# Token sums of a Strassen-like product: x1 and x2 in PSUM, issued in four parts behind the products of the chunk in front; modulation steps there left out or thinned

## The chip, the cores and the metric

The kernel runs on one core of a Trainium2 chip. The metric is the device time of one execution in microseconds (us). The engines are named as the profile names them: PE (TensorE, matmul; PEld its weight loads), DVE (VectorE), ACT (ScalarE), POOL (GpSimd) and SP (SyncE, which issues DMAs). Each engine runs its own instructions in a fixed order.

## The reference

Two layers of a generator over 512 latent tokens and 256 context tokens, model width 1024, all in float32. Each layer is a half SwiGLU feed-forward, a token mixer (neighbourhood attention in layer 0, windowed attention in layer 1), and a second half SwiGLU. Every sub-layer is modulated by shift, scale and gate that come from a conditioning vector, and ends in a layer norm.

```python
def modulate(h, shift, scale):
    return h * (1.0 + scale) + shift

def swiglu(u, w_in, w_out):
    a, v = jnp.split(u @ w_in, 2, axis=-1)
    return (jax.nn.silu(a) * v) @ w_out

def ffn_sublayer(h, shift, scale, gate, w_in, w_out, g, b):
    y = swiglu(modulate(h, shift, scale), w_in, w_out)
    return layer_norm(ALPHA * h + FFN_RES * gate * y, g, b)

for i in range(DEPTH):                       # DEPTH = 2
    m_lat = split(silu(c) @ w_mod[i] + b_mod[i], 9)      # and m_ctx from c_ctx
    h = ffn_sublayer(h, m[0], m[1], m[2], ffn_w_in[i, 0], ffn_w_out[i, 0], ...)
    ...                                      # mixer i, layer norm
    h = ffn_sublayer(h, m[6], m[7], m[8], ffn_w_in[i, 1], ffn_w_out[i, 1], ...)
```

The hidden width of a feed-forward is 2816.

## The kernel before, in words

Tokens lie along the free axis, features along the 128 partitions. A float32 value goes to PE as two parts, high and low (`uh`, `ul` for the activations, `wh`, `wl` for the weights, `gh`, `gl` for the gated product), and each product is three matmuls (`mm3`, L146 to L148).

There are four feed-forwards, `0a`, `0b`, `1a` and `1b`. The first three take 768 tokens in two groups, 512 and 256 wide; `1b` takes the 512 latent tokens in two groups of 256. A feed-forward is a loop over `NCH` = 11 chunks of 256 hidden columns. A chunk first computes `a` and `v` for its two column halves and its groups (function `av`: tiles `pa`, `pv`; SiLU on ACT; the product with `v` on DVE, L456; the split into `gh` and `gl`, L457 and L458), and then multiplies by `w_out` (function `down`: 16 tiles `pd`; each is added to the stream `z` by `accumulate`, L432 on DVE). Inside `1b` one of the eight stream tiles is called `zspare`.

Chunks 0 up to `s0` - 1 run in this plain way; `s0` is 3 in `0a` and 2 in the others. Chunks `s0` to 8 run as `seven`: a Strassen-like form with seven products (`p0` to `p6`) in place of eight. It needs sums of quarters of the weights (`quarters`, tiles `S`, POOL, L541, split by ACT L102 and POOL or DVE L104) and sums of quarters of the activations. The latter are made once for each feed-forward:

- `sums()`, at the top of chunk `s0` - 1. For each of four rows `j` it stores the odd half of `uh` and `ul` in DRAM (two DMAs on SP), then makes x1 (three DVE instructions, L490), x3 (three POOL instructions, L490) and x2 from x1 (two DVE instructions, L490). Each of the three is split by a copy on ACT (L511) and a subtraction on DVE (L512) into tiles `T`. x1, x2 and x3 lie in the scratch tiles `t2` in SBUF, of which there are six.
- `fourth()`, at the end of chunk `s0` - 1: two subtractions on POOL (L523), an addition on DVE (L524), a copy on ACT (L525) and a subtraction on DVE (L526) for each row, in place over the odd half of `uh` and `ul`.

Product `p2` needs x2, `p3` x1, `p5` x3, `p6` what `fourth()` leaves. A set of these sums is 32 DVE, 12 POOL and 12 ACT instructions in `sums()` and 8 of each in `fourth()`, of 384 columns each, in `1b` of 256.

PSUM has eight banks, two of them tagged `mm`, two `s`, two `c`, one `t`, one `o`. `av` uses `mm` and `c`. Downs of chunks 1 to 8 and the seven products take `mm`, `s` and `c` in turn (`next_bank`).

Beside the feed-forwards `0a`, `0b` and `1a` the modulation vectors of what follows are computed on DVE (`gemv_dve`, L198: one multiply-and-sum of 128x512 for each step, with its accumulator read). The steps wait in a list `bg`; `tick()` takes from it as many as `pace` says, four times in a plain chunk and 14 times in a `seven` chunk. `weight` says how much of the work a chunk gets:

```python
weight = [0] + [1.6] * (s0 - 1) + [1.0] * (NCH - 2 - s0)
each = sum(n + 1 for n, _ in bg) / (sum(weight) - 0.1)
pace[0] = each * weight[ci] / (4 if ci < s0 else 14)
```

`0a` has 193 such entries, `0b` 97, `1a` 130 and `1b` none. `each` is thus 21.2, 11.4 and 15.3 before.

The order of the instructions on each engine is not written out by hand. A planner takes them by program order, when their inputs and a free buffer are there by its own model of times, so that an instruction may be put ahead of an earlier one. `behind(x, y)` forbids this for two instructions of the same engine: `x` then stands after `y`. It does nothing where the engines differ. `last[0]` is the last accumulate, gated product or combining step on DVE that the program has issued so far; the modulation steps stand behind it.

Of the kernel before, what the change touches and what calls it, by code (L numbers as in the profile page):

```python
# [8 lines left out]
F32 = mybir.dt.float32  # L9
F32R = mybir.dt.float32r  # L10
# [3 lines left out]
ALU = mybir.AluOpType  # L14
# [4 lines left out]
P = 128  # L19
# [7 lines left out]
NCH = NF // 2  # L27
# [11 lines left out]
def hybrid_kernel(ctx: ExitStack, tc: tile.TileContext, h0, cc, crow, wmod, wmodt, bmod, lnp, wst,  # L39
                  rpbp, nmask, sinks, ropec, rmat, ident, wmask, out):  # L40
    nc = tc.nc
# [5 lines left out]
    dp = ctx.enter_context(tc.tile_pool(name="dp", bufs=1, space=DRAM))  # L47
    banks = {"mm": 2, "s": 2, "c": 2, "t": 1, "o": 1}

    def bank(tag, nm):  # L50
        return pp.tile([P, 512], F32, tag=tag, name=nm, bufs=banks[tag])

    def t2(nm, tag="t2"):
        return tp.tile([P, 512], F32, tag=tag, name=nm, bufs={"t2": 6, "ln": 2, "sl": 2}[tag])
# [25 lines left out]
    uh = [rp.tile([P, NT], F32R, name=f"uh{d}") for d in range(DT)]  # L80
    ul = [rp.tile([P, NT], F32R, name=f"ul{d}") for d in range(DT)]
# [27 lines left out]
    ph, phase_of = {}, [None, ExitStack()]  # L109
# [76 lines left out]
    bg, last, last_exp, wtq = [], [None], [None], [0]  # L186
# [36 lines left out]
    def tick():  # L223

        pace[1] += pace[0]
        while bg and pace[1] >= 1:
            pace[1] -= 1
            if next(bg[0][1], "end") == "end":
                bg.pop(0)
# [78 lines left out]
    def behind(x, y):  # L308

        if y is not None and x.ins.engine == y.ins.engine:  # L310
            tc.add_manual_dep(x.ins, y.ins.name, mybir.DependencyInfo(
                mybir.DependencyClass.NoSync, mybir.DependencyReason.DATA), reason="order")
# [123 lines left out]
    def ffn(nm, groups, gt, mid, post, units=(), opened={}, head=None, apart=None):  # L436
# [4 lines left out]
        def unit(slabs=False):  # L441
            return units.pop(0) if units else wunit(slabs)
# [34 lines left out]
        n2 = nb * P  # L477

        def half(t, h):

            return t[:, 0:nb * 256].rearrange("p (a s b) -> p s a b", s=2, b=P)[:, h]

        def as_half(t):
            return t.rearrange("p (a b) -> p a b", b=P)

        ts = [[[None, None] for _ in range(4)] for _ in range(3)]

        def op(eng, out, a, b, o):
            a, b = [half(y[0], y[1]).bitcast(F32) if isinstance(y, tuple) else as_half(y) for y in (a, b)]
            eng.tensor_tensor(out=as_half(out), in0=a, in1=b, op=o)  # L490

        def sums():


            saved = dp.tile([2, 4, P, n2], F32, name=f"sv{nm}")
            for j in range(4):
                for x, t in enumerate((uh, ul)):
                    nc.sync.dma_start(saved[x, j].rearrange("p (a b) -> p a b", b=P), half(t[j], 1).bitcast(F32))
                x1, x2, x3 = [t2(f"x{nm}_{j}_{i}")[:, 0:n2] for i in range(3)]
                k = j + 4  # L500
                op(nc.vector, x1, (uh[j], 1), (uh[j], 0), ALU.subtract)
                op(nc.vector, x1, x1, (ul[j], 1), ALU.add)
                op(nc.vector, x1, x1, (ul[j], 0), ALU.subtract)
                op(nc.gpsimd, x3, (uh[k], 1), (uh[j], 1), ALU.subtract)
                op(nc.gpsimd, x3, x3, (ul[k], 1), ALU.add)
                op(nc.gpsimd, x3, x3, (ul[j], 1), ALU.subtract)
                op(nc.vector, x2, (uh[k], 1), x1, ALU.subtract)
                op(nc.vector, x2, x2, (ul[k], 1), ALU.add)
                for i, x in enumerate((x1, x2, x3)):
                    hi, lo = [ph["T"].tile([P, 384], F32R, tag=f"T{i}{j}{y}", name=f"T{nm}_{i}_{j}{y}", bufs=1)[:, 0:n2] for y in "hl"]  # L510
                    nc.scalar.copy(hi, x)  # L511
                    nc.vector.tensor_tensor(out=lo, in0=x, in1=hi.bitcast(F32), op=ALU.subtract)  # L512
                    ts[i][j] = [as_half(hi), as_half(lo)]
            return saved

        def fourth():

            for j in range(4):
                x = t2(f"x{nm}_{j}_4")[:, 0:n2]
                k = j + 4  # L520
                for i, (a, b, o) in enumerate(((ts[1][j][0], half(uh[k], 0), ALU.subtract), (ts[1][j][1], half(ul[k], 0), ALU.subtract))):
                    y = x if i == 0 else t2(f"x{nm}_{j}_5")[:, 0:n2]
                    nc.gpsimd.tensor_tensor(out=as_half(y), in0=a.bitcast(F32), in1=b.bitcast(F32), op=o)  # L523
                nc.vector.tensor_tensor(out=x, in0=x, in1=y, op=ALU.add)  # L524
                nc.scalar.copy(half(uh[j], 1), as_half(x))  # L525
                nc.vector.tensor_tensor(out=half(ul[j], 1), in0=as_half(x), in1=half(uh[j], 1).bitcast(F32), op=ALU.subtract)  # L526

# [73 lines left out]
        if mid is not None:  # L601
            mid()
        gts.append(gt())
        late_downs = []
        s0 = 3 if opened else 2
        weight = [0] + [1.6] * (s0 - 1) + [1.0] * (NCH - 2 - s0)
        each = sum(n + 1 for n, _ in bg) / (sum(weight) - 0.1)
        for ci in list(range(NCH)) + [("r", NCH - 2)]:
            r = isinstance(ci, tuple)
            if not r and 0 < ci < NCH - 2:  # L610
                phase("T")
                pace[0] = each * weight[ci] / (4 if ci < s0 else 14)
                if ci == s0 - 1:
                    saved = sums()
            if not r and s0 <= ci < NCH - 2:
                gs = [[gp.tile([P, NT], F32R, tag="gs", name=f"g{x}{nm}_{ci}_{i}", bufs=6) for x in "hl"] for i in range(2)]

                def lagging(ci=ci, gs=gs, u=wpos[0] + 2):
                    w = wunit(again=u, adding=True)
                    if ci == NCH - 3:  # L620
                        restore(saved)
                    for g in ([(0, NL, 0)] if nb == 2 else groups):
                        down(w, f"{ci}", gs, g, True)

                for i in range(2):
                    seven(f"{nm}_{ci}_{i}", wpos[0] + i, *gs[i])
                    while i == 0 and late_downs:
                        late_downs.pop()()
                late_downs.append(lagging)
                wpos[0] += 3  # L630
                if ci == NCH - 3:
                    late_downs.pop()()
                if ci == NCH - 3:
                    pace[0] = 1
                    while bg:
                        tick()
                continue
            if ci == NCH - 2:
                phase("S")
            late = ci == NCH - 2  # L640
            if late:
                again = wpos[0]
            w = [wunit(again=again + i) if r else unit(i == 2 and (ci == NCH - 1 or ci == 0 and apart is not None)) for i in range(3)]
            cn = f"r{ci[1]}" if r else f"{ci}"
            gs = [[gp.tile([P, NT], F32R, tag="gs", name=f"g{x}{nm}_{cn}_{i}", bufs=6) for x in "hl"] for i in range(2)]

            def avs(*todo):
                for g, i in todo:
                    av(w[i], f"{cn}_{i}", g, *gs[i], opened.get((i, g)) if ci == 0 else None, 4 if late else 0)
                    if not r and 0 < ci < s0:  # L650
                        tick()

            def dn(g):
                down(w[2], cn, gs, g, not r and 0 < ci < NCH - 2)

            a, b = groups
            if r:
                avs((b, 0), (b, 1))
                dn(b)
                post(1)  # L660
            elif late:
                avs((a, 0), (a, 1))
                dn(a)
            elif ci == NCH - 1:
                avs((a, 0), (a, 1))
                dn(a)
                avs((b, 0), (b, 1))
                post(0)
                dn(b)
            elif ci == 0 and apart:  # L670
                apart()
                avs((head[0], 0), (head[0], 1))
                dn(head[0])
                avs(*[(g, i) for g in head[1:] for i in range(2)])
                for g in head[1:]:
                    dn(g)
            else:
                avs(*([(g, i) for g in head for i in range(2)] if ci == 0 else [(a, 0), (b, 0), (a, 1), (b, 1)]))
                dn(a)
                dn(b)  # L680
            if ci == s0 - 1:
                fourth()
            if mid is not None and ci == 1:
                bias_tables()
# [424 lines left out]
    with tc.tile_pool(name="pre", bufs=1) as fp:  # L1109
        open_av()  # L1110
        for q in range(4):
            pieces = []
            for i in range(2):
                t = fp.tile([P, 4, 512], F32, tag="wm", name=f"wm0_{q}_{i}", bufs=7)
# [196 lines left out]
```

## Time and profile before

| | |
|---|---|
| runs | 2860.72, 2865.42, 2865.66 us, median 2865.42 |
| profiled execution, its own time | 2863.12 us |
| span of the profiled execution | 2861.0 us |
| mean granted PE clock | 0.977 |
| busy: PE, DVE, POOL, ACT | 2716.4, 1820.9, 1675.4, 1218.0 us |
| HBM traffic | 322.15 MB, mean 113 GB/s |

In rows of instructions a group reads: line, engine, operation, out<-in tiles, shapes, count | busy us, mean ns of one | idle time of the engine before them, and what ended it. In rows of stretches, each engine's busy time in the stretch is followed by the number of its instructions, and the row ends with the granted PE clock, the share of the DMA engines and GB/s; where the row is for one line of the code, only the engines that run this line are named. In rows of waits stands who waited for whom, how many us in total, how often, and the longest. Buffer numbers are left out of tile names, so that the chunks of one feed-forward share a name and are told apart by time.

### The profile page before, as it was taken

To read this page: it belongs to the slowest core of one execution; us is meant where nothing else is said; L and a number is where in the kernel's file an instruction comes from. 1 tells how busy PE (TensorE), PEld (TensorE's weight loads), DVE (VectorE), ACT (ScalarE), POOL (GpSimd) and SP (SyncE) were. 2 spreads that over 40 slices of the span, in tenths; PEclk is the share of its full clock that TensorE was granted. 3 is DMA by queue.
4 is the path that set the end of the run, shared out by engine and by line. 5 is a ranking of instruction groups with operands and counts; after the bars stand their busy time and mean duration, and the time that the engine had idled before them with its cause. 6 is when DMAs were issued, how large, how long until landed. Compare 5 with 4: busy or idle time off the path is not lost. (4 is left out here: it accounts for less than half of the span.)

```text
span 2861.0 us, 48069 instructions
## 1 busy us (share of the span) xinstructions
PE 2716.4 (95%) x17122; PEld 2438.8 (85%) x17122; DVE 1820.9 (64%) x4122; ACT 1218.0 (43%) x2496; POOL 1675.4 (59%) x1488
## 2 busy tenths in 40 slices
PE   8999999999999979999999889999997999899997
PEld 5789999888888868899998779999886777789997
DVE  3597776375555677766553886666457767787744
ACT  4224433266446343333433424433336655444543
POOL 4547674475434445876644667676456545577763
PEclk9999999999999989999999999999999999999998
DMA  8465656232221213445452335656431111135562
GB/s 300 124 192 159 159 144 162 79 99 78 56 56 54 66 49 93 118 126 137 116 140 77 93 107 142 169 169 181 133 97 47 51 38 45 56 88 134 126 174 70
DMA packets 285871, 322.15 MB, mean 113 GB/s; under 512 B 28480, under 2 KB 174016, under 8 KB 284608
## 3 DMA queue, kind: packets, MB, share of 16 engines
q1 hardware_dynamic: 269792, 290.63, 34.5%
q0 software_dynamic: 15552, 28.32, 6.0%
q8 instruction: 135, 2.21, 0.3%
q14 instruction: 104, 0.85, 0.1%
q10 hardware_dynamic: 288, 0.14, 0.0%
HBM read 311.14 MB, written 12.25 MB: 113 GB/s over the span
## 5 line engine op out<-in xcount | busy, mean ns | idle before, releaser
L104 POOL TENSOR_TENSOR wl<-wr,wh 128x512 fp32r<-128x512 f32 x308 | 406.0, 1333 | 307.7 <-ACT wh L102 268.8
L104 POOL TENSOR_TENSOR wl_s<-S,wh_s 128x512 fp32r<-128x512 f32 x202 | 270.4, 1374 | 49.5 <-ACT wh_s L102 44.1
L102 ACT CAST wh<-wr 128x512 fp32r<-128x512 f32 x308 | 187.7, 621 | 228.6 <-DMA wr<-in_wst_dram 59.4
L102 ACT CAST wh_s<-S 128x512 fp32r<-128x512 f32 x216 | 132.1, 622 | 325.2 <-POOL S L541 80.9
L541 POOL TENSOR_TENSOR S<-wr,wr 128x512 f32<-128x512 f32 x108 | 147.5, 1366 | 172.7 <-DMA wr<-in_wst_dram 147.7
L198 DVE CUSTOM_DVE_ANT_0 jk<-wt,cb 128x512 f32<-128x512 f32 x278 | 185.3, 680 | 57.8 <-DMA wt<-in_wmodt_dram 56.2
L104 POOL TENSOR_TENSOR wl_a<-wr,wh_a 128x512 fp32r<-128x512 f32 x120 | 159.2, 1382 | 31.8 <-ACT wh_a L102 22.3
L102 ACT CAST wh_a<-wr 128x512 fp32r<-128x512 f32 x162 | 100.8, 623 | 133.5 <-PE pd1b L147 17.0
L432 DVE SCALAR_TENSOR_TENSOR z<-pd0b,gt,z 128x256 f32<-128x256 f32 (+1 forms) x176 | 102.7, 602 | 63.1 <-PE pd0b L148 62.9
L432 DVE SCALAR_TENSOR_TENSOR z<-pd1a,gt,z 128x512 f32<-128x512 f32 (+1 forms) x168 | 99.0, 620 | 41.1 <-PE pd1a L148 40.8
L432 DVE SCALAR_TENSOR_TENSOR z<-pd0a,gt,z 128x512 f32<-128x512 f32 (+1 forms) x168 | 98.0, 619 | 34.4 <-PE pd0a L148 34.2
L765 POOL TENSOR_SCALAR p<-p,l 128x512 f32<-128x512 f32 x64 | 44.3, 694 | 119.4 <-DVE l L863 111.0
L305 POOL TENSOR_SCALAR z<-z,ag_None,ab_None 128x256 f32<-128x256 f32 (+1 forms) x78 | 68.8, 888 | 67.0 <-DVE uh L291 65.3
L198 DVE CUSTOM_DVE_ANT_0 jk<-zspare,cb 128x512 f32<-128x512 f32 x138 | 92.7, 680 | 13.6 <-DMA zspare<-in_wmodt_dram 13.4
L765 POOL TENSOR_SCALAR pw<-pw,l 128x512 f32<-128x512 f32 (+1 forms) x64 | 40.9, 641 | 66.2 <-DVE l L1052 25.4
L541 POOL TENSOR_TENSOR S<-S,wr 128x512 f32<-128x512 f32 x54 | 77.2, 1430 | 4.2 <-DVE x0b L524 1.7
L541 POOL TENSOR_TENSOR S<-wr,S 128x512 f32<-128x512 f32 x54 | 76.5, 1416 | 4.0 <-DVE ul L526 0.6
L862 ACT ACTIVATE p<-s,m 128x512 f32<-128x512 f32 x64 | 44.1, 690 | 77.7 <-DVE m L860 72.7
L287 ACT ACTIVATE ufl<-z,bi_None,sc_None 128x256 f32<-128x256 f32 (+1 forms) x86 | 54.5, 657 | 34.3 <-DVE z L411 33.9
L432 DVE SCALAR_TENSOR_TENSOR z<-pd1b,gt,z 128x512 f32<-128x512 f32 (+1 forms) x98 | 56.5, 610 | 13.2 <-PE pd1b L148 11.0
L292 DVE TENSOR_TENSOR ul<-ufl,uh 128x256 fp32r<-128x256 f32 (+1 forms) x88 | 60.4, 696 | 0.9 <-ACT ufl L287 0.6
L146 PE MATMUL pd0a<-gh0a,wh 128*128 128x512 f32 (+1 forms) x144 | 50.3, 358 | 8.0 <-DVE z L432 7.8
(1462 smaller groups left out, 10701.1 us busy)
## 6 DMA issues: line engine op xcount, KB each, us to landing
wr<-in_wst_dram SPq DMA_DIRECT2D x524, 256.0 KB
wt<-in_wmodt_dram SPq DMA_DIRECT2D x160, 256.0 KB
zspare<-in_wmodt_dram SPq DMA_DIRECT2D x80, 256.0 KB
wr_0b<-in_wst_dram SPq DMA_DIRECT2D x42, 256.0 KB
wr_1b<-in_wst_dram SPq DMA_DIRECT2D x42, 256.0 KB
wr_2b<-in_wst_dram SPq DMA_DIRECT2D x42, 256.0 KB
wr_3b<-in_wst_dram SPq DMA_DIRECT2D x42, 256.0 KB
wm<-in_wmod_dram SPq DMA_DIRECT2D x8, 1024.0 KB
```

What stands on the lines that cost most here:

```text
L102: nc.scalar.copy(hi[:], src[:])
L104: eng.tensor_tensor(out=lo[:], in0=src[:], in1=hi[:].bitcast(F32), op=ALU.subtract)
L146: nc.tensor.matmul(ps, a[0], b[0], start=first, stop=False)
L198: x = nc.vector.tensor_tensor_reduce(out=junk[:], in0=w[:], in1=cb[st], scale=1.0, scalar=0.0, op0=ALU.mult, op1=ALU.add, accum_out=acc[:, ...
L287: nc.scalar.activation(uf[:, :n], zs, AF.Identity, scale=s1, bias=s2)
L292: return hi, nc.vector.tensor_tensor(out=lo, in0=uv, in1=uo.bitcast(F32), op=ALU.subtract)
L305: nc.gpsimd.tensor_scalar(out=zs, in0=zs, scalar1=prm[2][:, d:d + 1], scalar2=prm[3][:, d:d + 1], op0=ALU.mult, op1=ALU.add)
L432: last[0] = nc.vector.scalar_tensor_tensor(out=zt(d, c0, c1), in0=pd, scalar=gt[:, d, st:st + 1], in1=zt(d, c0, c1), op0=ALU.mult, op1=ALU ...
L541: nc.gpsimd.tensor_tensor(out=t[:], in0=a[:], in1=b[:], op=o)
L765: nc.gpsimd.tensor_scalar(out=p, in0=p, scalar1=r, scalar2=0.0, op0=ALU.mult, op1=ALU.add)
L862: last_exp[0] = nc.scalar.activation(p[:], ps[:], AF.Exp, bias=m[:, 0:1], scale=-1.0, accum_out=l[:, 0:1])
```

## The change

1. x1 and x2 lie in PSUM (banks `s`) and no more in `t2`; x3 stays in `t2`. In `fourth()` the sum lies in a bank `s` and its two inputs in `t2`.
2. `sums()` is called for one row at a time: row 0 at the top of chunk `s0` - 1, rows 1 to 3 after the first three `av` of this chunk. The 16 storing DMAs are issued together before row 0 (`save`).
3. The instructions of the sums on DVE stand behind `last[0]`.
4. Modulation steps: `weight` is 0 for chunk 1 in `0b` and `1a`; in `0a` it is 1.3 for chunk 1 and 0.7 for chunk 2, in place of 1.6 each. `each` becomes 24.4, 14.1 and 18.8 in `0a`, `0b` and `1a`, so that the later chunks take more.

```diff
@@ in ffn
         def op(eng, out, a, b, o):
             a, b = [half(y[0], y[1]).bitcast(F32) if isinstance(y, tuple) else as_half(y) for y in (a, b)]
-            eng.tensor_tensor(out=as_half(out), in0=a, in1=b, op=o)
-
-        def sums():
-            saved = dp.tile([2, 4, P, n2], F32, name=f"sv{nm}")
+            behind(eng.tensor_tensor(out=as_half(out), in0=a, in1=b, op=o), last[0])
+
+        def save(saved):
             for j in range(4):
                 for x, t in enumerate((uh, ul)):
                     nc.sync.dma_start(saved[x, j].rearrange("p (a b) -> p a b", b=P), half(t[j], 1).bitcast(F32))
-                x1, x2, x3 = [t2(f"x{nm}_{j}_{i}")[:, 0:n2] for i in range(3)]
+
+        def sums(j):
+            x1, x2 = [bank("s", f"x{nm}_{j}_{i}")[:, 0:n2] for i in range(2)]
+            x3 = t2(f"x{nm}_{j}_2")[:, 0:n2]
+            k = j + 4
+            op(nc.vector, x1, (uh[j], 1), (uh[j], 0), ALU.subtract)
+            op(nc.vector, x1, x1, (ul[j], 1), ALU.add)
+            op(nc.vector, x1, x1, (ul[j], 0), ALU.subtract)
+            op(nc.gpsimd, x3, (uh[k], 1), (uh[j], 1), ALU.subtract)
+            op(nc.gpsimd, x3, x3, (ul[k], 1), ALU.add)
+            op(nc.gpsimd, x3, x3, (ul[j], 1), ALU.subtract)
+
+            def split(i, x):
+                hi, lo = [ph["T"].tile([P, 384], F32R, tag=f"T{i}{j}{y}", name=f"T{nm}_{i}_{j}{y}", bufs=1)[:, 0:n2] for y in "hl"]
+                nc.scalar.copy(hi, x)
+                behind(nc.vector.tensor_tensor(out=lo, in0=x, in1=hi.bitcast(F32), op=ALU.subtract), last[0])
+                ts[i][j] = [as_half(hi), as_half(lo)]
+
+            op(nc.vector, x2, (uh[k], 1), x1, ALU.subtract)
+            op(nc.vector, x2, x2, (ul[k], 1), ALU.add)
+            split(0, x1)
+            split(1, x2)
+            split(2, x3)
+
+        def fourth():
+            for j in range(4):
+                x = bank("s", f"x{nm}_{j}_3")[:, 0:n2]
                 k = j + 4
...
-                for i, (a, b, o) in enumerate(((ts[1][j][0], half(uh[k], 0), ALU.subtract), (ts[1][j][1], half(ul[k], 0), ALU.subtract))):
-                    y = x if i == 0 else t2(f"x{nm}_{j}_5")[:, 0:n2]
-                    nc.gpsimd.tensor_tensor(out=as_half(y), in0=a.bitcast(F32), in1=b.bitcast(F32), op=o)
-                nc.vector.tensor_tensor(out=x, in0=x, in1=y, op=ALU.add)
+                ys = [t2(f"x{nm}_{j}_{i}")[:, 0:n2] for i in (4, 5)]
+                for i, t in enumerate((uh, ul)):
+                    nc.gpsimd.tensor_tensor(out=as_half(ys[i]), in0=ts[1][j][i].bitcast(F32), in1=half(t[k], 0).bitcast(F32),
+                                            op=ALU.subtract)
+                nc.vector.tensor_tensor(out=x, in0=ys[0], in1=ys[1], op=ALU.add)
                 nc.scalar.copy(half(uh[j], 1), as_half(x))
                 nc.vector.tensor_tensor(out=half(ul[j], 1), in0=as_half(x), in1=half(uh[j], 1).bitcast(F32), op=ALU.subtract)
...
-        late_downs = []
+        late_downs, js = [], [1, 2, 3]
         s0 = 3 if opened else 2
-        weight = [0] + [1.6] * (s0 - 1) + [1.0] * (NCH - 2 - s0)
+        weight = [0] + [1.3] * (s0 - 2) + [0.7 * (s0 - 2)] + [1.0] * (NCH - 2 - s0)
...
                 if ci == s0 - 1:
-                    saved = sums()
+                    saved = dp.tile([2, 4, P, n2], F32, name=f"sv{nm}")
+                    save(saved)
+                    sums(0)
...
                     if not r and 0 < ci < s0:
                         tick()
+                    if not r and ci == s0 - 1 and js:
+                        sums(js.pop(0))
```

More of the change, by code (lines that the diff above doesn't have):

```diff
@@ L498, in sums @@
                     nc.sync.dma_start(saved[x, j].rearrange("p (a b) -> p a b", b=P), half(t[j], 1).bitcast(F32))
-                x1, x2, x3 = [t2(f"x{nm}_{j}_{i}")[:, 0:n2] for i in range(3)]
[L500 to L513, printed above, removed]
@@ L514, in sums @@
-            return saved
+        def sums(j):
[18 more added lines that the diff above has]
+            split(2, x3)
@@ L516, in fourth @@
         def fourth():
             for j in range(4):
-                x = t2(f"x{nm}_{j}_4")[:, 0:n2]
+                x = bank("s", f"x{nm}_{j}_3")[:, 0:n2]
                 k = j + 4
-                for i, (a, b, o) in enumerate(((ts[1][j][0], half(uh[k], 0), ALU.subtract), (ts[1][j][1], half(ul[k], 0), ALU.subtract))):
-                    y = x if i == 0 else t2(f"x{nm}_{j}_5")[:, 0:n2]
-                    nc.gpsimd.tensor_tensor(out=as_half(y), in0=a.bitcast(F32), in1=b.bitcast(F32), op=o)
```

## The prediction

> **What bounds the kernel now.** I read the page first, then the windows of each stage, then what TensorE (PE) waits for, then the timeline of VectorE (DVE) in those places.
>
> ```profile
> PE 2716.4 (95%) x17122; PEld 2438.8 (85%) x17122; DVE 1820.9 (64%) x4122; ACT 1218.0 (43%) x2496; POOL 1675.4 (59%) x1488
> ```
>
> PE is the bound: only 2861.0 - 2716.4 = 145 us of the span have no matmul running. The change can win only where PE stands still or clocks low near the code it touches. The next view gives busy time by stretch: chunks 1 and 2 of `0a`, chunk 1 and then chunk 2 of `0b`, chunk 1 of `1a`, of `1b`; then the down products of one chunk in `0b`, `1a`, `1b` and of a later chunk in `1b`; last the worst stretch of `1a`.
>
> ```profile
> core 0: us, PE busy (x) PEld busy (x) DVE busy (x) ACT busy (x) POOL busy (x), PEclk, DMA share, GB/s
> 105.00:165.00 60.00, 52.45 (x286) 45.33 (x285) 57.28 (x109) 15.22 (x30) 42.95 (x33) 0.94 0.59 170
> 165.00:212.00 47.00, 46.59 (x267) 40.77 (x266) 43.09 (x115) 11.09 (x22) 21.74 (x17) 1.00 0.64 183
> 1120.00:1167.00 47.00, 40.36 (x220) 33.88 (x220) 46.84 (x91) 15.15 (x31) 33.80 (x28) 0.96 0.33 90
> 1167.00:1227.00 60.00, 59.07 (x338) 56.34 (x337) 37.60 (x86) 23.18 (x43) 48.30 (x40) 1.00 0.48 128
> 1680.00:1722.00 42.00, 42.00 (x258) 37.98 (x257) 33.95 (x84) 12.06 (x24) 29.19 (x22) 1.00 0.51 149
> 2506.00:2546.00 40.00, 33.99 (x259) 32.87 (x258) 38.91 (x61) 15.61 (x37) 32.64 (x29) 0.91 0.17 51
> ...
> 1138.60:1165.30 26.70, 20.06 (x98) 15.47 (x97) 26.70 (x53) 7.82 (x16) 20.20 (x16) 0.94 0.27 69
> 1702.20:1719.10 16.90, 16.90 (x98) 14.77 (x98) 16.39 (x32) 3.81 (x8) 14.95 (x12) 1.00 0.42 123
> 2521.90:2542.70 20.80, 14.79 (x98) 13.67 (x97) 19.78 (x33) 7.28 (x16) 16.89 (x15) 0.84 0.13 39
> 2572.80:2584.00 11.20, 11.20 (x51) 9.07 (x50) 7.54 (x13) 3.47 (x8) 9.80 (x8) 1.00 0.60 142
> ...
> 1636.00:1662.00 26.00, 16.47 (x72) 13.23 (x72) 25.94 (x29) 7.20 (x17) 22.64 (x18) 0.74 0.30 87
> ```
>
> See that DVE is full (57.28 of 60, 46.84 of 47, 38.91 of 40, 25.94 of 26) exactly where PE idles, and that the clean stretches have PE at 100% and clock 1.00. The same 16 down tiles of one chunk take 26.70 us in `0b` and 16.90 in `1a`: 9.8 us lost. In `1b` 20.80 against 11.20 (the same 24,576 columns in wider matmuls): 9.6 lost. In `0a` PE idles 60.00 - 52.45 = 7.55, in `1a` 26.00 - 16.47 = 9.53. What PE waits for there, a row each from the waits of 0a, 0b, 1a (two) and 1b:
>
> ```profile
> PE pd0a L146 <- DVE z L432: 7.5, 5, 3.0
> ...
> PE pd0b L146 <- DVE gl0b L458: 3.0, 1, 3.0
> ...
> PE pv1a L146 <- DVE gl1a L458: 6.1, 1, 6.1
> PE pd1a L146 <- DVE z L432: 3.5, 1, 3.5
> ...
> PE pd1b L146 <- DVE zspare L432: 5.0, 1, 5.0
> ```
>
> It waits for accumulates (`z`, L432) and for the split of the gated product (`gl`, L458): short DVE steps queued behind `sums()`. **Removable: 7.55 + 9.8 + 9.53 + 9.6 = 36.5 us.** With the lowered clock of the idle stretches of `0a` and `1a` (52.45 x 0.06 = 3.1 and 16.47 x 0.26 = 4.3) the ceiling is about 44.
>
> **Part 1: x1 and x2 in PSUM.** DVE instructions of these tiles (256 columns where the name ends in `1b`, else 384), by form:
>
> ```profile
> L490 DVE TENSOR_TENSOR x1a<-x1a,ul 128x384 f32<-128x384 f32 x12 | 11.6, 975 | 0.0
> L490 DVE TENSOR_TENSOR x0b<-uh 128x384 f32<-128x384 f32 x4 | 2.2, 548 | 0.0
> L570 DVE TENSOR_TENSOR p51a<-p51a,y1a 128x384 f32<-128x384 f32 x14 | 7.9, 567 | 1.8 <-DVE p51a L570 0.5
> L570 DVE TENSOR_TENSOR y1a<-p11a,y01a 128x384 f32<-128x384 f32 x14 | 7.8, 556 | 21.5 <-PE p11a L148 21.5
> L570 DVE TENSOR_TENSOR y1b<-p11b,y01b 128x256 f32<-128x256 f32 x14 | 5.8, 415 | 1.2 <-PE p11b L148 1.2
> ```
>
> With both inputs in SBUF the same shape takes 548 ns undisturbed and 975 on the mean; with one in PSUM 556, writing PSUM 567, and that beside a busy POOL too. Of a row's eight DVE steps six get one PSUM input; the first subtraction and the split of x3 keep two SBUF inputs. I price those at 0.95 (between 0.55 and the 975 mean, nearest the latter because POOL works beside them): 4 x (2 x 0.95 + 6 x 0.556) = 20.9 us a product set, 17.7 in `1b` (0.42 for 0.556). Before (L490, then L512, in `0b` early, `0b`, `1b`):
>
> ```profile
> 1077.00:1120.00 43.00, 8.38 (x10) 6.95 (x6) 0.97 0.36 99
> 1120.00:1167.00 47.00, 7.34 (x10) 7.32 (x6) 0.96 0.33 90
> 2506.00:2546.00 40.00, 9.02 (x10) 5.35 (x6) 0.91 0.17 51
> ...
> 1120.00:1167.00 47.00, 11.44 (x12) 0.96 0.33 90
> 2506.00:2546.00 40.00, 8.05 (x12) 0.91 0.17 51
> ```
>
> So `0b` paid 8.38 + 7.34 + 11.44 = 27.2 us of DVE, of which 8.38 lay early. In `fourth()` the final split gets a PSUM input too: 4 x (0.95 + 0.556) = 6.0 us, 5.5 in `1b`. Rows of L526 (`0a`, `0b`, `1a`, `1b`), then of L524 (`0b`, `1b`):
>
> ```profile
> 165.00:212.00 47.00, 4.48 (x4) 1.00 0.64 183
> 1120.00:1167.00 47.00, 3.54 (x4) 0.96 0.33 90
> 1680.00:1722.00 42.00, 4.55 (x4) 1.00 0.51 149
> 2506.00:2546.00 40.00, 4.24 (x4) 0.91 0.17 51
> ...
> 1120.00:1167.00 47.00, 3.70 (x4) 0.96 0.33 90
> 2506.00:2546.00 40.00, 3.45 (x4) 0.91 0.17 51
> ```
>
> **Part 2: behind `last[0]`, in four parts.** DVE's 32 steps can no longer run ahead of the previous chunk's last accumulate; the ten early ones in `0b`, and those that filled 105 to 165 in `0a` and 1636 to 1662 in `1a`, move into the chunk that emits them. POOL's steps are on another engine, where the edge does nothing; the 16 saving DMAs keep their place ahead of the chunk's loads: nothing for either. New waits: a row's x1 and x2 hold both banks `s`, so DVE stands until ScalarE has copied them; what queues behind is accumulates. Bounds: a small gain, if the two scratch tiles a row that come free let POOL start its weight sums sooner; 0, if other DVE work fits between; 4 x 0.556 = 2.2 us a product set, if each row waits out a copy about as long as a DVE step. I take 0 here, since what is ready fits between, and leave 2.2 to the kept stalls below.
>
> **Part 3: modulation steps.** They leave chunk 1 of `0b` and `1a`, and thin from 34 to 17 in chunk 2 of `0a` (24.4 x 0.7, plus some 3 late ones: 20). L198 in `0b`, `0a`, `1a`; half the count are accumulator reads:
>
> ```profile
> 1120.00:1167.00 47.00, 13.20 (x40) 0.96 0.33 90
> 165.00:212.00 47.00, 30.52 (x93) 1.00 0.64 183
> 1680.00:1722.00 42.00, 17.68 (x54) 1.00 0.51 149
> ```
>
> A step costs 0.66 us. The later chunks take about 3 more each, 2 us of DVE, covered by PE's products, since DVE is busy 37.60 of 60.00 us in such a chunk (row 1167 above); uncovered it would be 2 us on each of 20 chunks. I charge 1 us in all.
>
> **DVE's load against PE's time in the chunk.** `0a`: 43.09 - 30.5 + 20 x 0.66 + 20.9 + 6.0 - 4.48 = 48.2, against 47 and the first two products' 4.2 (the third needs x2): 94%. `0b`: 46.84 - 13.2 - 18.8 + 20.9 + 6.0 - 7.2 = 34.5 against 47 - 9.8: 93%. `1a`: 33.95 - 17.7 + 20.9 + 6.0 - 4.55 = 38.6 of 42: 92%. `1b`: 38.91 - 17.1 + 17.7 + 5.5 - 7.7 = 37.3 against 40 - 9.6 + 2.9 = 33.3: over by 4. Late next are accumulates again, in a less crowded queue. Kept stalls, my estimate from these loads: 3.5, 2, 2 and 5. **Sum: 36.5 - 12.5 - 1 = 23 us off the profiled execution's 2863.1 (2.3 under the median of the runs): 2840.**
>
> [...]
>
> **Rivals.**
>
> *All of it.* If neither kept stall nor thinning costs anything and the clock stays up: 2863.1 - 44 + 1 = 2820. For it: chunk 1 of `1a` already runs 16.90 us of downs with DVE at 16.39. Against: `1b`'s overload.
>
> *Weight splits cap it.* In `0b` POOL makes the third product's low half at 1161.3 and PE's third product starts at 1169.5; POOL's part of `fourth()` (L523, last row) lies just ahead:
>
> ```profile
> L104 POOL TENSOR_TENSOR wl_s<-S,wh_s x4: 1308/1598/1614, 1161.3 to 1166.9; 128x512 fp32r<-128x512 f32 x4
> ...
> L146 PE MATMUL p20b<-T0b_0h,wh_s x1: 332/332/332, 1169.5 to 1169.5; 128*128 128x384 f32 x1
> ...
> 1120.00:1167.00 47.00, 9.47 (x8) 0.96 0.33 90
> ```
>
> PE may come about 7 us sooner, not 9.8, unless POOL does too: 2.8 lost in `0b`. In `0a` and `1a` those 9.5 us of POOL now follow late sums: some 4 each. 2840 + 11 = 2851.
>
> *Stalls only move.* DVE blocks the downs of the next chunk as long as it did those of this one in `0a`, `1a` and `1b`; only `0b`, which sheds steps, gains 5: 2858, no change that counts.
>
> *Slower: the two banks `s`.* Downs and the seven products rotate over `mm`, `s`, `c`; a product on `s` waits while `fourth()` holds both. Price: one row of it, two POOL steps, 9.47/8 x 2 = 2.4 us; three of seven products, four times: 29 us, 2840 + 29 = 2869. It decides from 6 us a product set. Against: other banks' work can go first.
>
> [...]
>
> **How the numbers follow.** Forecast 0.47, all of it 0.18, weight splits 0.13, only moved 0.09, banks 0.10, dear PSUM 0.03. A change of 0.2% (5.7 us) is about what this kernel's runs can tell. Faster: 0.47 + 0.18 + 0.13 + 0.03 = 0.81; same 0.09; slower 0.10. The range 2819 to 2860 leaves out the slower case and half of the best one; the likeliest alone: 2830 to 2848.
>
> **What would show it.** Right: sums on DVE only after each previous chunk's last accumulate; six of eight steps near 0.56; the downs of `0b` near 18 us and of `1b` near 16; PE without wait between 105 and 165; no L198 in chunk 1 of `0b` and `1a`. Wrong: PE waiting for `s` banks or `T` tiles at the first products, POOL's splits ending late there, accumulates late in chunk 2 of `0a`, or new stalls in the later chunks.

## The result and the profile after

| | before | after |
|---|---|---|
| median of the runs shown together | 2867.18 us (2860.72 to 2870.52, 6 runs) | 2880.34 us (2876.84 to 2884.35, 6 runs) |
| profiled execution, span | 2863.12, 2861.0 us | 2880.27, 2878.5 us |
| granted clock | 0.977 | 0.975 |

The ratio is 1.0048 with a 95% interval of 1.0035 to 1.0062: the changed kernel is 13 us slower. The forecast was 2840, with a range of 2819 to 2860.

The same line of the page; then stretch 105 to 165 of `0a`, and three stretches that end at the first seven product of `1a` and `1b` and 3 us before that of `0b` (in the order `0b`, `1a`, `1b`):

```profile
PE 2719.7 (94%) x17122; PEld 2441.6 (85%) x17122; DVE 1776.5 (62%) x4122; ACT 1212.1 (42%) x2496; POOL 1652.1 (57%) x1488
```

```profile
core 0: us, PE busy (x) PEld busy (x) DVE busy (x) ACT busy (x) POOL busy (x), PEclk, DMA share, GB/s
105.00:165.00 60.00, 52.35 (x279) 44.76 (x277) 36.57 (x89) 11.84 (x21) 22.68 (x20) 0.89 0.63 184
...
1131.50:1161.20 29.70, 29.70 (x169) 25.99 (x168) 28.09 (x53) 7.38 (x16) 12.80 (x10) 1.00 0.20 62
1691.00:1710.60 19.60, 19.60 (x121) 17.48 (x120) 13.98 (x25) 2.86 (x6) 3.05 (x3) 1.00 0.00 1
2521.00:2543.80 22.80, 22.80 (x195) 22.80 (x194) 20.11 (x47) 5.88 (x16) 8.62 (x9) 1.00 0.16 47
```

DVE lost 44 us of work (1820.9 to 1776.5), and in these 20 to 30 us of `0b`, `1a` and `1b` PE stands nowhere: 100% busy at clock 1.00. So much came as forecast. But PE has 14.2 us more idle in the whole span than before (158.8 against 144.6), and stretch 105 to 165 of `0a` is as it was: 52.35 busy of 60.00 (52.45 before), with DVE now at 36.57.

Where the idle time went shows when each feed-forward is cut at its first product, the first matmul of `p0` in its first `seven` chunk. "In front" is from the first matmul of its `pa` to there, "behind" from there to its last down. PE's idle time in us, in front / behind:

| kernel | `0a` | `0b` | `1a` | `1b` | all four |
|---|---|---|---|---|---|
| before | 10.7 / 2.9 | 13.6 / 0.9 | 17.7 / 2.9 | 8.0 / 2.0 | 50.0 / 8.7 |
| after | 10.4 / 13.4 | 7.1 / 7.5 | 7.2 / 14.8 | 1.4 / 12.4 | 26.1 / 48.1 |
| e1 (below) | 12.6 / 9.6 | 7.3 / 0.8 | 8.0 / 9.6 | 3.2 / 5.1 | 31.1 / 25.1 |
| e8 (below) | 11.3 / 2.6 | 9.7 / 0.1 | 8.0 / 7.3 | 3.6 / 4.9 | 32.6 / 14.9 |

The change takes 24 us of idle time off in front and adds 39 behind. What is waited for from 105 to 165 (first row) and around the first product of `0a`, `0b`, `1a`, `1b`:

```profile
PE pd0a L146 <- DVE z L432: 7.6, 2, 7.1
...
POOL x0a L530 <- DVE x0a L532: 17.4, 1, 17.4
...
PE p10a L146 <- DVE ul L534: 4.9, 1, 4.9
...
POOL x0b L530 <- ACT y0b L590: 16.7, 1, 16.7
...
PE p20b L146 <- ACT wh_s L102: 7.4, 1, 7.4
...
POOL x1a L530 <- DVE x1a L532: 15.7, 1, 15.7
...
PE p21a L146 <- ACT wh_s L102: 2.2, 1, 2.2
...
POOL x1b L530 <- DVE x1b L532: 12.6, 1, 12.6
...
PE p21b L146 <- ACT wh_s L102: 2.8, 1, 2.8
```

Around each first product POOL stands 13 to 17 us before row 3 of `fourth()` (rows counted from 0; the subtractions are L530 after the change, the add is L532, the split L534). In `0b` the profile names ACT's L590, which ended within 0.1 us of the add. PE then waits 4.9 + 7.4 + 2.2 + 2.8 = 17.3 us. The last three are for `wh_s`, the split of the weight sums that POOL makes late. The 4.9 in `0a` is for a bank: `p1` reads nothing that `fourth()` writes, but by the turn of `next_bank` it lies in a bank `s`, and it starts at 217.44, when the split of row 2 has read that bank. The timeline of `1a`, POOL and then DVE, shows why POOL stands:

```profile
1710.72 1.02 POOL L530 TENSOR_TENSOR x1a<-T1a_3h,uh 128x384 f32<-128x384 f32 x1 [15.71 <-DVE x1a L532]
1711.70 1.03 POOL L530 TENSOR_TENSOR x1a<-T1a_3l,ul 128x384 f32<-128x384 f32 x1
1713.60 1.53 POOL L549 TENSOR_TENSOR S<-wr,wr 128x512 f32<-128x512 f32 x1 [0.86 <-DVE x1a L532]
...
1705.77 2.02 DVE L432 SCALAR_TENSOR_TENSOR z<-pd1a,gt,z 128x512 f32<-128x512 f32 x4 [1.22 <-PE pd1a L148]
...
1709.42 0.48 DVE L432 SCALAR_TENSOR_TENSOR z<-pd1a,gt,z 128x256 f32<-128x256 f32 x1 [0.22 <-PE pd1a L148]
1710.01 0.57 DVE L532 TENSOR_TENSOR x1a<-x1a,x1a 128x384 f32<-128x384 f32 x1
```

The add L532 now writes a bank `s`, and those banks go round with the downs. It runs only behind the accumulates (L432) of the last downs, at 1710.01. Until then rows 0 to 2 of `fourth()` keep their inputs, two scratch tiles each, all six. POOL has no tile for row 3, and its weight sums (L549), which feed the first products, are queued behind that row.

In the table below the net of a block is how much longer than before it takes in the profiled execution, front and behind together: from the first matmul of its `pa` to its last down. After: `0a` +13.0, `0b` -5.0, `1a` +5.0, `1b` +4.0.

### The profile page after: what moved, and what is told of

It reads as the page before. It is cut to its first block, busy times and chain, and to the rows that moved or that the text cites. A ratio compares the mean times of both kernels' runs of the same rounds, so it can differ in the third digit from the quotient of the medians.

```text
span 2878.5 us, 48120 instructions
## 1 busy us (share of the span) xinstructions
PE 2719.7 (94%) x17122; PEld 2441.6 (85%) x17122; DVE 1776.5 (62%) x4122; ACT 1212.1 (42%) x2496; POOL 1652.1 (57%) x1488
## 5 line engine op out<-in xcount | busy, mean ns | idle before, releaser
L549 POOL TENSOR_TENSOR S<-wr,wr 128x512 f32<-128x512 f32 x108 | 146.3, 1354 | 164.7 <-DMA wr<-in_wst_dram 149.8
L432 DVE SCALAR_TENSOR_TENSOR z<-pd0b,gt,z 128x256 f32<-128x256 f32 (+1 forms) x176 | 103.2, 604 | 75.6 <-PE pd0b L148 75.2
L432 DVE SCALAR_TENSOR_TENSOR z<-pd1a,gt,z 128x512 f32<-128x512 f32 (+1 forms) x168 | 99.8, 621 | 57.1 <-PE pd1a L148 56.7
L432 DVE SCALAR_TENSOR_TENSOR z<-pd0a,gt,z 128x512 f32<-128x512 f32 (+1 forms) x168 | 98.8, 622 | 48.1 <-PE pd0a L148 47.9
L549 POOL TENSOR_TENSOR S<-S,wr 128x512 f32<-128x512 f32 x54 | 76.3, 1412 | 2.7
L549 POOL TENSOR_TENSOR S<-wr,S 128x512 f32<-128x512 f32 x54 | 75.0, 1389 | 3.1
L432 DVE SCALAR_TENSOR_TENSOR z<-pd1b,gt,z 128x512 f32<-128x512 f32 (+1 forms) x98 | 57.0, 611 | 14.9 <-PE pd1b L148 12.6
L146 PE MATMUL pd0a<-gh0a,wh 128*128 128x512 f32 (+1 forms) x144 | 50.6, 362 | 7.6 <-DVE z L432 7.6
```

What stands on the lines that cost most here:

```text
L146: nc.tensor.matmul(ps, a[0], b[0], start=first, stop=False)
L432: last[0] = nc.vector.scalar_tensor_tensor(out=zt(d, c0, c1), in0=pd, scalar=gt[:, d, st:st + 1], in1=zt(d, c0, c1), op0=ALU.mult, op1=ALU ...
L549: nc.gpsimd.tensor_tensor(out=t[:], in0=a[:], in1=b[:], op=o)
```

## The experiments

Twelve kernels, each timed beside the kernel before (medians 2868.52, 2867.95 and 2867.69 us in the three sets). The ratio is against before.

| kernel | us | ratio, 95% interval | net `0a` | `0b` | `1a` | `1b` |
|---|---|---|---|---|---|---|
| after | 2880.3 | 1.0048 [1.0035, 1.0062] | +13.0 | -5.0 | +5.0 | +4.0 |
| e1 fourth in scratch | 2861.8 | 0.9983 [0.9969, 0.9997] | +13.2 | -9.3 | -5.4 | -3.7 |
| e2 after, old weights | 2895.1 | 1.0098 [1.008, 1.0115] | +19.4 | +1.5 | +3.7 | +6.2 |
| e3 e1, old weights | 2879.5 | 1.0036 [1.0022, 1.005] | +11.5 | -1.2 | +0.7 | -3.4 |
| e4 before, new weights | 2874.7 | 1.002 [1.0008, 1.0032] | +8.6 | -5.9 | +2.6 | +1.1 |
| e5 inputs in `ln`, 1b | 2880.6 | 1.0039 [1.0024, 1.0055] | +14.9 | -1.9 | +0.7 | +1.4 |
| e6 e1, x in SBUF | 2903.1 | 1.0129 [1.0113, 1.0146] | +19.9 | +3.8 | +8.1 | +6.6 |
| e7 e1, no edge | 2858.8 | 0.9972 [0.9959, 0.9985] | +12.8 | -12.1 | -1.9 | -4.9 |
| e8 e1, 0a as before | 2843.8 | 0.9916 [0.9896, 0.9936] | -2.0 | -10.8 | -7.3 | -4.6 |
| e9 e8, no edge | 2853.9 | 0.995 [0.9932, 0.9967] | -0.9 | -11.6 | +0.7 | -2.8 |
| e10 e8, fourth in bank | 2862.7 | 0.9983 [0.997, 0.9996] | -1.8 | -3.3 | +2.4 | +5.8 |
| e11 e8, PSUM in 0a | 2849.4 | 0.9935 [0.9918, 0.9951] | +5.6 | -11.5 | -4.9 | -1.4 |
| e12 e8, half weight | 2858.5 | 0.9965 [0.9952, 0.9979] | +1.8 | -5.5 | -4.0 | -0.8 |

The net wanders where the code of a block is the same: `1b` in e1, e8, e11, e12 is -3.7, -4.6, -1.4, -0.8, `0a` in e8, e9, e10, e12 is -2.0, -0.9, -1.8, +1.8. A difference under some 4 us in one block says nothing. (The expectation of e8 below has -2.2 for `1b` in e1; the trace gives -3.7.)

**e1: fourth()'s sum in its own scratch tile.**

```
-                x = bank("s", f"x{nm}_{j}_3")[:, 0:n2]
+                x = ys[0]
-                nc.vector.tensor_tensor(out=x, in0=ys[0], in1=ys[1], op=ALU.add)
+                nc.vector.tensor_tensor(out=x, in0=x, in1=ys[1], op=ALU.add)
```

> The changed kernel with the sum of fourth() back in a scratch tile t2 in SBUF, in place over its first input, as before the change; all else as changed. Theory A (scratch held): the addition L532 stands until a bank s is free, after the last downs, and its inputs hold all six t2 tiles meanwhile, so POOL idles 12.6 to 17.4 us in each of the four product sets and the weight sums for the first two seven-product blocks are late. Then these POOL waits go, the blocks after the first keep the 14.6 us (1b: 10.0) of the kernel before, some 35 to 45 us come back, and the time is 2835 to 2850, faster than before by 0.6 to 1.1%. Theory B (the thickened modulation in the later chunks is what costs): the time stays at 2870 or more and the blocks stay late by as much.

2861.8, 18.5 us less than after, though not the full size that was expected. The waits of `1a` over the same stretch begin with these, and the one of POOL for L532 is no longer among them:

```profile
ACT wh_s L102 <- POOL S L549: 8.6, 7, 2.8
ACT uh L533 <- DVE x1a L532: 4.7, 1, 4.7
```

PE waits for no `wh_s` there any more, the nets of `0b`, `1a` and `1b` turn negative, and of the 48.1 us that PE stood behind the first products 23 are gone. The net of `0a` stays at +13.2: there is a second cost.

**e2: the changed kernel with the weights of before, and e4: the kernel before with the new ones.**

```
-        weight = [0] + [1.3] * (s0 - 2) + [0.7 * (s0 - 2)] + [1.0] * (NCH - 2 - s0)
+        weight = [0] + [1.6] * (s0 - 1) + [1.0] * (NCH - 2 - s0)
```

> The changed kernel with the modulation weights of before (1.6 in each plain chunk after the first, 1.0 later). Theory A (scratch held by fourth()): POOL waits of 12 to 17 us stay in all four sets, the time stays within 2872 to 2888; 1b, which has no modulation, loses its 16 us as in the changed kernel. Theory B (thickened modulation): the time falls below 2860.

> The kernel before with only the new modulation weights (none in chunk 1 of 0b and 1a, fewer in chunk 2 of 0a, more later). Theory A: the crowded chunk 1 of 0b gives back part of its 9.8 us, the seven-product chunks of 1a lose some 6 to 9 us and 0a some 7: within 0.3% of before, 2860 to 2875. Theory B: slower by most of the loss of the change, 2875 or more.

Neither theory had e2: it is 15 us slower than after. With its steps back in the chunk in front, DVE ends the sums later, and downs of PE also wait for the last split (L514), which still reads a bank `s` (their weight loads 3.5 us in `0a` and 3.7 in `1a`). By itself the thinning is a loss: e4 is 6.2 us slower than before, of which `0a` holds most (+8.6). PE's waits there (255 to 330) were 1.9 and 0.8 us before; in e4:

```profile
PE pd0a L146 <- DVE z L432: 7.1, 2, 4.6
```

and DVE's, in the same kernel, between 212 and 330, with the reload of the `cb` vectors at half time (ACT makes them at 300 and 304; before, at 263 and 265, and DVE didn't wait for them):

```profile
DVE jk L198 <- ACT cb L211: 8.7, 2, 5.9
DVE jk L198 <- DMA zspare<-in_wmodt_dram: 7.8, 2, 5.8
```

A step that waits for its data holds the accumulate behind it; this is read from the waits and wasn't tried. So the new weights cost 6 us by themselves, and the changed kernel is 15 us slower still without them.

**e5: in `1b` the inputs of fourth() take the two `ln` tiles, the sum stays in a bank.**

```
-                ys = [t2(f"x{nm}_{j}_{i}")[:, 0:n2] for i in (4, 5)]
+                ys = [t2(f"x{nm}_{j}_{i}", "ln" if nb == 2 else "t2")[:, 0:n2] for i in (4, 5)]
```

> The changed kernel; in 1b alone the two inputs of the sum in fourth() lie in the two tiles of tag ln, which nothing else uses there, and not in t2; the sum itself stays in a bank s. Theory A: the addition L532 stays as late as in the change, but POOL can make the weight sums S of 1b in time since t2 is free: 1b's first two blocks keep 10.0 us each and the time falls by 8 to 16 us, to 2864 to 2872, with 0a, 0b and 1a unchanged. Rival (the bank itself, a late fourth() or the order on DVE, is what delays): 1b stays as late and the time stays at 2880.

No gain that counts: 2880.6, and `1b` +1.4 against +4.0. The waits from 2540 to 2600:

```profile
POOL S L549 <- DMA wr<-in_wst_dram: 7.3, 2, 4.0
ACT uh L533 <- DVE x1b L532: 6.1, 4, 2.7
...
PE p61b L146 <- ACT uh L533: 4.5, 3, 2.3
```

POOL is free of row 3, but the sum is as late as it was, and PE now waits for `uh`, which is made of it. In `1b` to free the scratch is not enough while the add waits for its bank. How the loss is shared between the held scratch and the late sum itself was not tried in the other blocks.

**e3: e1 with the weights of before.** The edit is that of e2 on e1.

> The changed kernel with fourth()'s sum kept in its scratch tile (as in e1, 2861.8) and the weights of before: modulation steps stay in the chunk in front. Theory A, the moved modulation steps cost what they cost in e4 (its behind-part of 0a lost 11.6 us, of 1a 4.3): this loses less behind the first product in 0a and 1a, and the time comes out 5 to 12 us under e1, 2850 to 2857. Theory B, the four parts need a thin chunk (as e2 against the changed kernel, 15 us worse): the sums end late, PE waits for the last T tiles and for the first weight splits, and the time is 10 to 20 us over e1, 2872 to 2882.

2879.5, 17.7 us over e1: theory B. Four parts need the thin chunk, with or without the held scratch. `0a` stays bad under either weights (+11.5), so the thinning isn't the whole of its loss. Here a bank of x1 and x2 does cost: behind the first product of `0a` a down waits 5.0 us for one that the last split still reads (`PE pd0a L146 <- DVE T0a_3l L514`; 2.3 us in e11, none in the changed kernel).

**e6: e1 with x1 and x2 in SBUF again.**

```
-            x1, x2 = [bank("s", f"x{nm}_{j}_{i}")[:, 0:n2] for i in range(2)]
+            x1, x2 = [t2(f"x{nm}_{j}_{i}")[:, 0:n2] for i in range(2)]
```

> e1 with x1 and x2 in scratch tiles of SBUF again, so that only the four parts, the edge and the weights are left of the change. Theory A, the PSUM operands carry the gain in front: the six steps a row go from about 0.57 to 0.95 us, 24 x 0.38 = 9 us of DVE a product set, and two more scratch tiles a row are held, so the gain in front of the first product (4.3, 13.6, 15.8, 9.6 us in e1) falls by 5 to 9 us a set: 2880 to 2895. Theory B, the order (four parts behind the last accumulate) carries it and DVE has room: within 5 us of e1, 2857 to 2867.

2903.1, 41 us over e1, more than theory A said. The groups of L490 by form, first e6, then the changed kernel (its stretch 1640 to 1720):

```profile
L490 DVE TENSOR_TENSOR x1a<-x1a,ul 128x384 f32<-128x384 f32 x12 | 13.2, 1107 | 0.1
```

```profile
L490 DVE TENSOR_TENSOR x1a<-x1a,ul 128x384 f32<-128x384 f32 x12 | 6.8, 563 | 0.3
L490 DVE TENSOR_TENSOR x1a<-uh 128x384 f32<-128x384 f32 x4 | 3.3, 818 | 0.1
```

The same twelve instructions take 13.2 us with both inputs in SBUF and 6.8 with one in PSUM; the first subtraction, which has two SBUF inputs in both, took 818 ns in the changed kernel and 1227 in e6. In all, DVE is busy 1822.1 us in e6 against 1781.3 in e1, 41 us more, as much as the kernel loses. But e6 also holds two more scratch tiles a row, and the two effects were not told apart.

**e7: e1 without the ordering edge.**

```
-            behind(eng.tensor_tensor(out=as_half(out), in0=a, in1=b, op=o), last[0])
+            eng.tensor_tensor(out=as_half(out), in0=a, in1=b, op=o)
...
-                behind(nc.vector.tensor_tensor(out=lo, in0=x, in1=hi.bitcast(F32), op=ALU.subtract), last[0])
+                nc.vector.tensor_tensor(out=lo, in0=x, in1=hi.bitcast(F32), op=ALU.subtract)
```

> e1 without the ordering edge that puts the sums behind the last accumulate; parts, PSUM tiles and weights stay. Theory A, the edge does the work: without it DVE runs the first part ahead of accumulates again and PE waits for z and gl in the chunk in front: 2868 or more. Theory B, the four places of issue do it and the edge is idle: 2858 to 2866, and the first products of all four blocks start within 2 us of those of e1.

2858.8, not told apart from e1: the intervals overlap. The blocks differ, though: in front of its first product `1a` takes 10 us longer than in e1, and its later part gives 7 back.

**e8: e1 with `0a` as before** (`opened` is set in `0a` alone: sums in one block, SBUF tiles, no edge, old weights).

```
+        def edge(x):
+            if not opened:
+                behind(x, last[0])
...
+            x1, x2 = [(t2(f"x{nm}_{j}_{i}") if opened else bank("s", f"x{nm}_{j}_{i}"))[:, 0:n2] for i in range(2)]
...
+        weight = [0] + ([1.6] * (s0 - 1) if opened else [0]) + [1.0] * (NCH - 2 - s0)
...
                     sums(0)
+                    while opened and js:
+                        sums(js.pop(0))
```

> e1, but with block 0a as before the change (sums in one block, scratch tiles of SBUF, no edge, old weights); the change holds in 0b, 1a and 1b alone. Theory A, what the change costs in 0a is its own (net +13.2 us from the start to the end of 0a in e1, against -9.3, -5.4 and -2.2 in the others): the 13 us go, 2868.5 - 17 = 2852, between 2845 and 2856. Theory B, the losses wander (0b to 1b take over what 0a had lost, as a queue or the weight stream sets the pace): within 4 us of e1, 2858 to 2866.

2843.8, ratio 0.9916 [0.9896, 0.9936]: faster than both kernels, and theory A to the size: `0a` is back at -2.0, the other three keep what they had. PE's row of the page:

```profile
PE 2706.2 (95%) x17122; PEld 2432.2 (86%) x17122; DVE 1790.5 (63%) x4122; ACT 1213.6 (43%) x2496; POOL 1659.8 (58%) x1488
```

Idle time is 2840.2 - 2706.2 = 134 us, against 144.6 before and 158.8 after.

**e10: e8 with fourth()'s sum in a bank `s` in 0b, 1a and 1b.**

```
-                x = ys[0]
+                x = ys[0] if opened else bank("s", f"x{nm}_{j}_3")[:, 0:n2]
```

> The changed kernel with block 0a as before; fourth()'s sum stays in a bank s in 0b, 1a and 1b. If the two costs, that of 0a and that of the held scratch, are separate, this is e8 plus what e1 saved behind the first products of 0b, 1a and 1b (11.6 - 4.3, 21.0 - 10.3, 15.5 - 7.4, less what the front gives back, together 18): 2843.8 + 18 = 2862, between 2856 and 2868. If the held scratch cost its time mainly through 0a, 2844 to 2852.

2862.7, as forecast, with the wait of the changed kernel back in `1a`:

```profile
POOL x1a L533 <- DVE x1a L536: 15.5, 1, 15.5
```

The four kernels make a square, and the two costs add:

| | sum in a bank `s` | sum in scratch | difference |
|---|---|---|---|
| `0a` changed | 2880.3 (after) | 2861.8 (e1) | 18.5 |
| `0a` as before | 2862.7 (e10) | 2843.8 (e8) | 18.9 |
| difference | 17.6 | 18.0 | |

**e9, e11, e12: e8 without the edge, with PSUM operands in `0a`, and with half the modulation steps in front.**

```
e9   -            if not opened:
     -                behind(x, last[0])
     +            pass
e11  +            x1, x2 = [bank("s", f"x{nm}_{j}_{i}")[:, 0:n2] for i in range(2)]
e12  +        weight = [0] + ([1.6] * (s0 - 1) if opened else [0.8]) + [1.0] * (NCH - 2 - s0)
```

> e8 (2843.8) without the ordering edge in 0b, 1a and 1b too. e7 against e1 was 3 us less, within the spread of both. Theory A, the edge is idle: 2840 to 2847. Theory B, the edge costs by holding back early subtractions: under 2839. Theory C, it protects accumulates: over 2848; in e7, PE lost 7.8 us early in 1a (1643) on z, which e1 did not.

> e8 with x1 and x2 in the banks s in 0a as well; the sums of 0a still in one block, no edge, weights of before. Theory A, PSUM operands are cheaper everywhere (0.57 against some 0.95 us): DVE gets 24 x 0.4 = 9 us back in the chunk in front of 0a, and PE's 7 us of waits for z between 105 and 150 shrink: 2836 to 2841. Theory B, in one block the two banks are a chain of copies, and the downs that rotate over s wait: over 2848.

> e8 with the modulation weight 0.8 instead of 0 in the chunk in front of 0b and 1a (1.6 before the change). Theory A, the moved steps cost in the later chunks of 1a (7.5 us behind the first product in e8): half of that comes back, and the front, whose DVE had 8 per cent of slack, loses less: 2838 to 2843. Theory B, the front chunk has no room beside four parts: as e3 against e1, where the old weights cost 18 us, half of it without 0a: 2848 to 2855.

e9: 2853.9, 10 us over e8, of which 8.0 lie in `1a`, with this among the waits from 1615 to 1660 (e8 has no wait of PE for `z` as long there):

```profile
PE pd1a L146 <- DVE z L432: 7.8, 1, 7.8
```

It speaks for theory C, that the edge protects the accumulates of `1a`; but the interval touches that of e8, and e7, which loses the same time in front of `1a`, lost nothing in total. The edge's worth is open, from nothing to some 10 us.

e12: 2858.5, past theory B: half of the old weight in front loses 15 us. Some 9 of it lie in `0b` and `1a` (5.3 and 3.3); the rest is in blocks of the same code and stays unexplained. In `0b` (first line) and `1a` POOL's part of `fourth()` waits for late splits:

```profile
POOL x0b L533 <- ACT T0b_2h L517: 8.2, 1, 8.2
...
POOL x1a L533 <- ACT T1a_2h L517: 8.3, 1, 8.3
```

e11: 2849.4 against 2843.8 with touching intervals, but `0a` alone goes from -2.0 to +5.6. The cheaper operands (the twelve steps of L490 in `0a` took 855 ns each before and 563 in the changed kernel) bring a loss there. In its waits from 105 to 150, first, and in those of e3 by DVE alone, behind:

```profile
DVE jk L198 <- DMA wt<-in_wmodt_dram: 11.9, 2, 10.2
...
PE pd0a L146 <- DVE z L432: 7.9, 2, 7.4
```

```profile
DVE jk L198 <- DMA wt<-in_wmodt_dram: 11.5, 2, 9.8
```

The timeline of the changed kernel, DVE and then SP's queue, says where `wt` was:

```profile
127.95 0.68 DVE L198 CUSTOM_DVE_ANT_0 jk<-zspare,cb 128x512 f32<-128x512 f32 x1
128.55 0.09 DVE L198 DVE_READ_ACCUMULATOR2_ANT ga<- 128x1 f32 x1
138.59 0.69 DVE L198 CUSTOM_DVE_ANT_0 jk<-wt,cb 128x512 f32<-128x512 f32 x1 [9.95 <-DMA wt<-in_wmodt_dram]
...
117.97 9.17 SPq L796 DMA_DIRECT2D yd<-xd  x10
128.00 0.88 SPq L195 DMA_DIRECT2D wt<-in_wmodt_dram  x1
129.44 2.06 SPq L796 DMA_DIRECT2D yd<-xd  x2
132.37 0.33 SPq L195 DMA_DIRECT2D wt<-in_wmodt_dram  x1
```

Sixteen copies `yd<-xd`, which `bias_tables()` issues at the end of chunk 1, stand in SP's queue; fourteen of them leave from 115.07 on, and the load of `wt` behind them at 128.00. It lands near 138.5. Its tile was free from 124.8 on, when the DVE step that began at 124.13 had read it, so the queue explains some 3 us of the wait at most; the load itself took 10.5 us, and why is not shown. Before, with sums to do, DVE takes these steps only from 142.48 on. Without them it reaches the next one at 128.6, stands 9.95 us, and the accumulates behind it make PE wait 7.1 us. A kernel with those copies moved wasn't tried.

This wait isn't the loss of `0a`. Between 105 and 165 PE waits for `z` as long as it did: 7.6 us after, 7.5 before, 8.2 in e8. The late load can explain why `0a` gains nothing in front; what it loses, it loses behind.

## Why the prediction was wrong, point by point

**What bounds the kernel: right for the front of three blocks in four.** Less its kept stalls the forecast took 4.0, 7.8, 7.5 and 4.6 us from `0a`, `0b`, `1a` and `1b`, 24 in all. The changed kernel took 0.3, 6.5, 10.5 and 6.6 us of PE's idle time from their fronts, 24 too. That the total fits is luck in part: `1a` and `1b` gave 5 us more than forecast and `0a` nothing. There the 7.55 us was counted as removable because DVE was full; the loads that DVE's next steps need weren't looked at. "PE without wait between 105 and 165" failed on that. The miss itself lies behind the first products: 39 us more idle time, where the sum had 1.

The nets of e8, -10.8, -7.3 and -4.6 in `0b`, `1a` and `1b`, look like the forecast's 7.8, 7.5 and 4.6, and that too is luck in part. In front e8 takes 14.6, 15.8 and 9.4 us less than before, partly because some downs now run behind the first product; behind, it takes 3.8, 8.5 and 4.8 more. In `1a` PE waits 7.1 us for `gl` and `z` behind the first product, where it waited 2.9 before; those chunks now have more modulation steps on DVE.

**Part 1: the price was right, the place of one bank was not asked.** 0.556 us was forecast for a step with a PSUM input, 563 ns measured (L490, `1a`); 0.95 us for one with two SBUF inputs, 818 ns measured; e6 shows what the place of x1 and x2 is worth, 41 us, the scratch they would hold included. No run shows PSUM operands to be dear (0.03 among the chances): a step with one as input took these 563 ns, the one with none 818 in the same kernel and 548 where it was fastest (`0b` before). But the bank of `fourth()` was priced as DVE time alone, 6.0 us a set. What it waits for was not asked, although it rotates with the downs.

**Part 2: the step that failed.** "I take 0 here, since what is ready fits between", with a small gain as the other end. The bounds were made for x1 and x2, whose banks cost nothing visible in the changed kernel. The wait of `fourth()`'s sum for its bank is in no term of the sum. The add behind the downs keeps six scratch tiles, POOL stands 13 to 17 us and PE 17.3 in all; taking the bank away gains 18.5 or 18.9. "Two scratch tiles a row that come free" was true, and turned round by who holds the six. The rival "the two banks `s`" (0.10) had the place, the banks and the sign right. Its direction came true in `0a`, where `p1` waits 4.9 us for a bank that `fourth()` holds. In the other three blocks `p2` is the product on `s`, and there `wh_s` came last (in `0b` by about half a us). What the rival lacked is the other direction, `fourth()` waiting for the downs, which makes both late. "Weight splits cap it" (0.13) named the last wait, `wh_s`, with its 7 us in `0b`, and not its cause. The signs of being wrong had it: PE waiting for `s` banks at the first products, and POOL's splits late there.

**Part 3: charged 1 us, costs 6 by itself.** e4 is 6.2 us slower than before [0.08%, 0.32%]. The charge was DVE time, covered by PE; what came was steps that stand for `zspare` and `cb` with an accumulate behind them. It bought more than was forecast, too: 15 and 17.7 us with the four parts (e2, e3), 14.7 in e12, part of that outside the blocks it concerns.

**The sum.** 2840 forecast, 2843.8 in e8. The 40 us up to 2880 are 18.5 for `fourth()`'s bank, 18.0 for the changed `0a`, and 4 left. That e8 comes so near is no proof of the sum, as e8 leaves `0a` out. Of `0a` it is shown that several parts lose there alone: weights +8.6 (e4), PSUM operands +7.6 against e8 (e11), parts, operands and edge with old weights +11.5 (e3). These don't add to the +13 of all together. Three waits of PE are seen behind its first product: 4.9 us for `fourth()`'s bank (after, and gone in e1); 7 to 8 us between 255 and 330 with the new weights (after, e1, e4; 2.7 before, 3.1 in e3); and 5.0 us for the last split's bank with the old ones (e3). How these and what else the parts do share the 13 us is open.

## What to carry to other kernels

A temporary that is moved into a rotating bank takes on the wait of that bank's last user (here POOL stood 13 to 17 us behind it): ask when the bank is free, what stays held until then, and which engine's queue stands behind it. Relieving a full engine helps only as far as its next instruction has its data (here DVE stood 9.95 us for `wt`): look at the loads of the steps it will reach earlier, and at the queue that issues them. A change made alike in four places is tried in each of them; in e1 three gained 18 us together and one gave 13 back.

## What of the hardware was not expected

DVE steps with two SBUF inputs got slower still in e6: 1107 ns on the mean in `1a` for the form that took 975 before and 563 with one PSUM input. Whether POOL's steps beside them are the reason was not worked out. A row of splits in `0b` shows the difference within one kernel, where 3 x 918 ns hold two PSUM-fed splits and that of x3:

```profile
L514 DVE TENSOR_TENSOR T0b_0l<-x0b,T0b_0h 128x384 fp32r<-128x384 f32 x3 | 2.8, 918 | 0.0
L514 DVE TENSOR_TENSOR T0b_2l<-x0b,T0b_2h 128x384 fp32r<-128x384 f32 x3 | 1.7, 550 | 0.0
```

If the two PSUM-fed ones took 550 as in the second row, that of x3 took 3 x 918 - 2 x 550 = 1654 ns; the timeline has 1.64, 0.56 and 0.55 us for the three. And the issue of a DMA from SP's queue isn't free: ten `yd<-xd` took 9.17 us of it, up to 3 us of them waits for earlier copies (2.9 us in all from 112 to 133).
